# First sums ahead of the K/V matmuls, later norm sums, last stores in pairs of blocks: three small moves in a decoder layer on eight cores

## The chip, the cores and the metric

The kernel runs on the 8 cores of one Trainium2 chip (two dies, cores 0 to 3 and 4 to 7). Each core computes 1024 of the 8192 positions and does not talk to the others. The metric is the device time of the slowest core in microseconds (us). A run is called slow when one die is clearly longer at a lower granted TensorE clock.

A difference by dies below about half a us should not be read as more than the spread between chips. Most runs list the span and granted clock of every core. Where a size is quoted below "by dies", it is the mean span of the four cores of a die whose cores all had a granted clock of 0.997 or more in that execution (an undisturbed die), averaged over all such dies. For the kernel before this is 6568.96 us over 62 dies on several chips (62 of the 96 dies of its 48 executions with a list of cores; the other 34 had a lower clock), with a standard deviation of 0.44 us; the mean differed by at most 0.6 us from chip to chip. Dies of executions whose other die was slow are counted too, as long as their own clock was full.

## The reference, cut to what matters

```python
h = rms_norm(x, g0); z = h @ w_in            # q, k, v, pool input, two gates
...                                          # attention, pooling, output projection, conv MLP
ple_gate = sigmoid(rms_norm(x, g4) @ w_ple_gate)
x = x + rms_norm(ple_gate * (p @ w_ple), g5) # the last stage
```

Two pieces matter here. At the start, each core needs the sums of squares of its x (the norm) and the K and V projections. In the last stage, `rms_norm` needs a sum over all 4096 features before any output can be scaled, so this sum and what follows it stand at the very end.

## The kernel before: the parts that matter

One helper records every operation, in program order, onto one queue per engine; each engine then works through its queue in order. Waits are derived from the buffers read and written. So an operation that is queued early, and has to wait, holds up all that stands behind it on its engine: on VectorE the K/V eviction ran at 62.99 us behind a gain multiply that had stood 16.82 us for its x load (core 5, shown below).

The start. Positions come in 4 slices of 4 loads each (`g` counts 16 loads; the eight sum matmuls of load `g` are called one sum below, so the fifth sum is that of the first load of the second slice). `prep` squares a load on ScalarE and multiplies it by the gain on VectorE; `stat` sums the squares on TensorE (8 matmuls with ones); `kv` does 32 matmuls.

```python
def load_x(n):        # the sixth load waits until the last K/V weight piece has landed
    O("sp", "dma_start", [wkv[3][3].b] if n == 5 else [], [xsub[i].b], ...)
...
prep(0); prep(1)
for g in range(4 * NSL):
    s, q = g // 4, g % 4
    if q == 0:
        kv(g, 0, 4); stat(g); kv(g, 4, 8)
    else:
        stat(g); kv(g)
    prep(g + 2)
    if g < 4:
        ...                                  # two memsets on VectorE
    ...
    if q == 3:
        kv_evac(s)                           # VectorE takes K and V of the slice out of PSUM
```

The last stage. Matmuls are recorded one by one, and every so often one step of a side queue is recorded between two of them: `due` grows by 1/side for each matmul, and a step is taken when it reaches 1. The first half of the positions (512 wide) runs as 32 blocks, then the second half for 24 blocks, then the last 8 blocks as two quarters of 256 (`half_job`, h = 0 and 1). When a part is done, its norm is put into the side queue. Its first step is a sum on TensorE, which needs the last block's gate, product and square from VectorE and ScalarE.

```python
# end of the first half, in the last block's eviction
B.side.extend(last_A(acc_rstd(acc, ((0, 512),))))     # first step: norm sum, then 32 output steps
...
# last block of a quarter: gate, product, square, then
B.due = 0
B.side.extend(last_B(h, last_rstd(h), (t, ap, f)))    # first step: norm sum, Ln, Exp, scale, 3 copies
...
# the last quarter's output, by groups of 4 blocks
for i in range(2):
    O("dve", "tensor_tensor", [R.b, x.b], [R.b], ...)  # add the residual to two blocks
put(g)()                                               # store 4 blocks, 512 KB
...
for eng, b in final_waits:                             # at the end SyncE waits once for every store
    for k, v in b.w.items(): fin.append((eng, k, v))
```

The softmax here doesn't subtract the row's maximum and nothing guards it: scores larger than these inputs give would overflow.

## Time and profile before

| | us |
|---|---|
| time, first three runs | 6624.95, 6634.72, 7356.29 (slow) |
| profiled run, slowest core (5) | 6572.5 |
| TensorE busy | 6497.6 |
| wait for K/V weights at the start (core 5) | 30.8 |
| wait for VectorE before the fifth sum | 7.7 |
| wait before the first half's norm sum | 2.6 |
| wait before the third quarter's norm sum | 1.0 |
| last large matmul to the end | 29 |

The page of core 5: busy time of the engines, and the chain of work that ended last, by engine.

```profile
PE 6497.6 (99%) x41466; PEld 4044.5 (62%) x41466; DVE 2040.5 (31%) x2713; ACT 894.0 (14%) x1397; POOL 1355.0 (21%) x2554
...
PE 98%; DMA 1%; DVE 1%; issue 0%; ACT 0%; POOL 0%; DVEq 0%; ACTq 0%; POOLq 0%; SPq 0%
```

TensorE is the bound (99% busy, 98% of the chain), so only its gaps can be won. The timeline of the first 64 us (start, duration, engine, instruction, count, and in brackets the idle time before and what ended it):

```profile
32.03 3.37 PE L145 MATMUL ps<-sb_arena 128*128 128x296 bf16 x13 [6.19 <-DMA sb_arena<-w_in]
...
35.19 1.25 PE L145 MATMUL ps<-sb_arena,sb_ones_b 128*128 128x296 bf16 x8
...
58.24 2.36 DVE L145 TENSOR_SCALAR sb_arena<-sb_arena,sb_cf 128x296 bf16<-128x296 f32 x8 [16.82 <-DMA sb_arena<-xs]
...
62.99 4.61 DVE L145 TENSOR_TENSOR sb_arena<-ps,sb_arena 128x296 bf16<-128x296 f32 x10
...
63.54 2.13 PE L145 MATMUL ps<-sb_arena,sb_ones_b 128*128 128x296 bf16 x8 [7.71 <-DVE sb_arena L145]
```

The eight sums of the first load (35.19) run after the weights have come. The fifth sum (63.54) waits for the K/V eviction (62.99), which stands in VectorE's queue behind a gain multiply that waits for the sixth x load (58.24).

```profile
6295.00:6300.00 5.00, 3.44 (x16) 1.36 (x14) 1.38 (x2) 1.22 (x2) 1.61 (x3) 1.00 0.52 142
6300.00:6305.00 5.00, 3.95 (x10) 1.52 (x11) 0.69 (x1) 3.36 (x5) 0.54 (x1) 0.72 0.08 32
6305.00:6310.00 5.00, 5.00 (x23) 2.21 (x22) 2.91 (x5) 0.00 (x0) 1.07 (x2) 0.94 0.64 174
```

TensorE is empty for 2.61 us, and after that the granted clock of the stretch is 0.72: the 39 matmuls at 6301.98 took 10.27 us, where 39 at 0.215 us would be 8.4 (between 6240 and 6270 us, at full clock, two starts are 0.216 us apart on the mean). Two more sums:

```profile
6276.27 1.02 PE L145 MATMUL ps<-sb_arena,sb_ones_f 128*128 128x512 f32 x2
...
6483.09 0.67 PE L145 MATMUL ps<-sb_arena,sb_ones_f 128*128 128x256 f32 x2 [0.30 <-DVE sb_arena L145]
```

The sum at 6483.09 us is the first sum of the last 8 blocks.

The two quarters and the last block, on TensorE and VectorE:

```profile
6514.90 0.27 PE L145 MATMUL ps<-sb_arena,sb_ones_b 128*128 128x256 bf16 x1 [1.04 <-ACT sb_arena L145]
...
6520.57 0.27 PE L145 MATMUL ps<-sb_arena,sb_ones_b 128*128 128x256 bf16 x1
...
6549.13 0.70 DVE L145 COPY sb_arena<-sb_arena 128x256 f32<-128x256 f32 x3 [0.59 <-ACT sb_arena L145]
6549.93 18.80 DVE L145 TENSOR_TENSOR sb_arena<-sb_arena 128x1024 f32<-128x1024 f32 x24
```

Then the stores: issue of the last 8 and their time to landing, from the view of the output tensor after 6550 us.

```profile
L145 SPq DMA_DIRECT2D out<-sb_arena x8: 372/372/373, 6553.6 to 6568.9; - x8
...
DMA to landing us min/median/max: 3.0/3.0/3.3
```

### The profile page before, as it was taken

Reading aid. Unit: us, or ns where it says so; the run is one execution under the profiler, and the core shown is the slowest. Engines: PE = TensorE matmul, PEld = TensorE weight load, DVE = VectorE, ACT = ScalarE, POOL = GpSimd, SP = SyncE. Lnnn points to the kernel's source line nnn. Section 1 sums busy time; section 2 is a strip of 40 time slices with the busy share of each in tenths; the row PEclk is TensorE's granted clock in tenths of the full one; section 3 lists DMA queues with packets and bytes.
Section 4 is the critical chain, followed back from the end, with each engine's and each line's share of the span. In section 5 each row is a group of like instructions: output and inputs, shape, how many; then the busy total and the mean of one; then the engine's idle time right before and its main releaser. Section 6 shows DMA issues by size and latency. Waiting matters only on the chain.

```text
span 6572.5 us, 105521 instructions; the slowest of 8 cores (6566.5 to 6572.5 us)
## 1 busy us (share of the span) xinstructions
PE 6497.6 (99%) x41466; PEld 4044.5 (62%) x41466; DVE 2040.5 (31%) x2713; ACT 894.0 (14%) x1397; POOL 1355.0 (21%) x2554
## 2 busy tenths in 40 slices
PE   7999999999999999999999999999999999999998
PEld 5666666666665685866644566665456666544445
DVE  4443111111111236433300133332013333335654
ACT  3640000000001233000000000000000000013433
POOL 1111111111112332211111111111111111233333
PEclk9999999999999999999999999999999999999999
DMA  8568777777776678677799977446774544578888
GB/s 194 83 92 119 117 114 113 119 122 117 116 117 178 178 215 247 144 110 110 110 153 160 152 114 108 77 77 125 160 144 77 77 76 76 129 218 278 240 250 264
DMA packets 387829, 931.69 MB, mean 142 GB/s; under 512 B 50192, under 2 KB 89360, under 8 KB 381584
## 3 DMA queue, kind: packets, MB, share of 16 engines
q0 software_dynamic: 292576, 726.30, 62.2%
q1 hardware_dynamic: 94336, 197.94, 9.2%
q8 instruction: 339, 5.55, 0.3%
q14 instruction: 146, 1.20, 0.1%
q10 hardware_dynamic: 432, 0.70, 0.1%
HBM read 1318.44 MB, written 206.61 MB: 232 GB/s over the span
## 4 chain that ended last, share of the span: by engine, by line
PE 98%; DMA 1%; DVE 1%; issue 0%; ACT 0%; POOL 0%; DVEq 0%; ACTq 0%; POOLq 0%; SPq 0%
PE ps L145 98%; DVE sb_arena L145 1%; DMA sb_arena<-w_in 1%; ACT sb_arena L145 0%; POOL sb_arena L145 0%; DMA sb_wr<-b_pg 0%; DMA sb_arena<-xs 0%; DVEq L144 0%; ACT L145 0%; DVEq L133 0%; ACTq L144 0%; ACT sb_warm L145 0%; POOLq L144 0%; SPq L144 0%; POOLq L170 0%
## 5 line engine op out<-in xcount | busy, mean ns | idle before, releaser
L145 PE MATMUL ps<-sb_arena,sb_wr 128*128 128x512 bf16 (+5 forms) x40000 | 6370.4, 321 | 0.5 <-DMA sb_wr<-b_pg 0.3
L145 PEld LDWEIGHTS ps<-sb_arena,sb_wr 128*128 128x128 bf16 x40000 | 3905.1, 98 | 2381.7 <-issue 7.8
L145 DVE TENSOR_TENSOR sb_arena<-ps,sb_arena 128x512 f32<-128x512 f32 (+12 forms) x936 | 683.9, 733 | 3855.6 <-PE ps L145 3677.0
L145 ACT ACTIVATE sb_arena<-sb_arena 128x512 f32<-128x512 f32 (+11 forms) x727 | 501.8, 693 | 4545.4 <-DVE sb_arena L145 4437.6
L145 DVE TENSOR_TENSOR sb_arena<-sb_arena 128x512 f32<-128x512 f32 (+8 forms) x687 | 545.0, 815 | 512.0 <-ACT sb_arena L145 477.2
L145 POOL DMA_DIRECT2D sb_wr<-w_up x608 | 321.9, 529 | 1748.2 <-PE ps L145 1681.2
L145 DVE SCALAR_TENSOR_TENSOR sb_arena<-sb_arena,sb_cf 128x1024 f32<-128x1024 f32 (+4 forms) x512 | 546.2, 1067 | 40.8 <-DVE sb_arena L145 0.9
L145 POOL DMA_DIRECT2D sb_wr<-w_in x384 | 204.0, 532 | 1242.4 <-PE ps L145 1151.2
L145 POOL DMA_DIRECT2D sb_wr<-w_down x256 | 135.5, 529 | 666.1 <-PE ps L145 639.0
L145 ACT ACTIVATE sb_arena<-ps 128x512 bf16<-128x512 f32 (+8 forms) x299 | 162.8, 545 | 709.9 <-PE ps L145 696.9
L145 PE MATMUL ps<-sb_arena 128*128 128x296 bf16 (+4 forms) x1216 | 180.0, 267 | 33.9 <-DMA sb_arena<-w_in 30.8
L145 POOL DMA_DIRECT2D sb_wr<-b_out x256 | 137.4, 537 | 333.1 <-PE ps L145 309.0
L145 DVE TENSOR_SCALAR sb_arena<-sb_arena,sb_cf 128x1024 f32<-128x1024 f32 (+3 forms) x320 | 183.2, 602 | 59.2 <-DMA sb_arena<-xs 25.7
L145 POOL DMA_DIRECT2D sb_wr<-b_pg x288 | 154.6, 537 | 223.0 <-PE ps L145 195.5
L145 POOL DMA_DIRECT2D sb_wr<-b_down x256 | 137.4, 537 | 273.9 <-PE ps L145 236.6
L145 PEld LDWEIGHTS ps<-sb_arena 128*128 128x128 bf16 (+1 forms) x1216 | 113.6, 98 | 89.7 <-issue 51.0
L145 ACT ACTIVATE sb_arena<-sb_arena,sb_cf 128x512 bf16<-128x512 f32 (+3 forms) x224 | 146.3, 653 | 11.2 <-ACT sb_arena L145 2.0
L145 POOL DMA_DIRECT2D sb_wr<-b_up x160 | 86.1, 538 | 202.4 <-PE ps L145 189.9
L145 ACT ACTIVATE sb_arena<-ps,sb_cf 64x386 f32<-64x386 f32 (+3 forms) x112 | 69.9, 624 | 250.4 <-PE ps L145 247.9
L145 DVE TENSOR_TENSOR sb_arena<-sb_arena,sb_cb 128x512 bf16<-128x512 bf16 (+1 forms) x192 | 64.2, 335 | 45.7 <-ACT sb_arena L145 39.1
L145 POOL DMA_DIRECT2D sb_wr<-w_bp x64 | 33.8, 528 | 190.8 <-PE ps L145 190.8
L145 POOL DMA_DIRECT2D sb_wr<-w_ba x64 | 34.2, 534 | 171.8 <-PE ps L145 171.8
(32 smaller groups left out, 256.3 us busy)
## 6 DMA issues: line engine op xcount, KB each, us to landing
sb_wr<-w_up POOLq DMA_DIRECT2D x608, 256.0 KB, 4.0
sb_wr<-w_in POOLq DMA_DIRECT2D x384, 256.0 KB, 5.6
sb_wr<-b_pg POOLq DMA_DIRECT2D x288, 256.0 KB, 5.0
sb_wr<-b_out POOLq DMA_DIRECT2D x256, 256.0 KB, 3.0
sb_wr<-w_down POOLq DMA_DIRECT2D x192, 256.0 KB, 5.5
sb_wr<-b_down POOLq DMA_DIRECT2D x192, 256.0 KB, 3.7
sb_wr<-b_up POOLq DMA_DIRECT2D x160, 256.0 KB, 3.5
b_out<-w_out POOLq DMA_DIRECT2D x32, 1024.0 KB, 12.3
```

Source lines behind the costliest of these rows:

```text
L145: inst = getattr(engine, fn[0])(**fn[1])
```

## The change

Its intent: to use the empty time at the start for the first sums, to keep TensorE from waiting at two norm sums of the last stage, and to shorten the landing of the last store.

```diff
-            if q == 0:
+            if q == 0 and s > 0:
                 kv(g, 0, 4)
                 stat(g)
                 kv(g, 4, 8)
@@ end of the first half
+                    B.side.append(idle)
                     B.side.extend(last_A(acc_rstd(acc, ((0, 512),))))
@@ last block of a quarter
-                    B.due = 0
+                    B.due = -0.6
@@ stores
-            def put(g):
+            def put(g, i=0, n=4):
...
-                    O("sp", "dma_start", [R.b, tok], [b], dma=f"out{g % 8}",
-                      out=out_d[4 * g:4 * g + 4, :, c0:c0 + HW]..., in_=R.v)
+                    O("sp", "dma_start", [R.b, tok], [b], dma=f"out{(2 * g + i // 2) % 8}",
+                      out=out_d[f0:f0 + n, :, c0:c0 + HW]..., in_=R.v[:, i:i + n, :])
...
-                        put(g)()
+                        put(g, 0, 2)()
+                        put(g, 2, 2)()
```

`idle` is an empty step: it costs one turn of the side queue, 13 matmuls there.

## The prediction

> **What bounds the kernel.** TensorE. The page gives PE 6497.6 of 6572.5 us (99%), and the chain that ended last is 98% PE. PE is empty mainly at the two ends that the change touches: waits of 38.5 us near the start, and 29 us after the last large matmul (6543.1 us in the timeline). 2% would be 130 us.
>
> **First slice.** The waits of PE in 0 to 150 us are 30.8 us for the K/V weights (4 waits) and one of 7.7 us for VectorE. The first 8 sum matmuls now run at 34.9 to 36.2 us (1.25 us), after the weights of the fourth column block have landed (32.0 us). Their squares are ready by 13.5 us, so the change puts them into empty time, near 14 us. That frees 1.2 us of PE between 32 and 49.8 us. I expect it to be lost: the chain runs through the landing of the last weight piece (49.8 us), which releases the sixth x load, landing at 58.0 us, then VectorE's gain multiply, two memsets and the K/V eviction, and only then the next sums (63.54 us). Gain 0, at most 0.5 us.
>
> **Norm sums queued later.** (a) The sum of the first half waits 0.30 us for VectorE (6483.09 us). One empty step, 13 matmuls of 0.215 us, covers it: gain 0.3 us. (b) The sum of the third quarter waits 1.04 us for ScalarE (6514.90 us). Starting at -0.6 means 28 matmuls instead of 17 before it, 1.25 us more: the wait goes. But the chain behind it (Ln, Exp, three copies, the gate with a table load, square) does not start earlier, and the next-but-one sum needs that square (19.85 to 20.27 us). So I expect a new wait of about 0.8 us at the sum near 6520.5. From there on VectorE sets the pace: per block gate 0.42, gap 0.68, multiply plus two queued steps 2.7 to 2.8 us, 3.78 us on average against 3.76 of PE. One queued step fewer fits before the end (13 instead of 14 after the start), so the last gate comes up to 1.1 us earlier, but that step (1.13 us) is done after it, where 0.59 us was idle: net 0.5 us.
>
> **Stores in pairs.** Both halves still wait for both adds, so no byte leaves earlier, and the last 1 MB already moves at about 320 GB/s (3.3 us). SyncE issues 8 more stores (0.37 us each, hidden behind VectorE's 18.8 us of tail) and ends with 56 instead of 48 store waits at 0.05 us each, started 0.45 us later: this list (2.8 us) may then outlast the landing by about 0.3 us. Cost 0 to 0.5 us.
>
> **Sum.** 0.3 + 0.5 - 0.3, about 0.5 to 1 us less, 0.01%, below the spread between fast runs (6624.95 and 6634.72 us; 6574 us profiled). Predicted 6633 us, range 6580 to 6665; chances 0.02 faster, 0.96 same, 0.02 slower.
>
> **What would show it.** Right: sums near 14 us, yet PE's VectorE wait still ends near 63.5 us; no wait at the two moved sums, a wait of 0.5 to 1 us two sums later; copies of the last quarter's norm within 1 us of their old place; stores of 256 KB and a list of waits at the end. Wrong: a K/V eviction or last landing a microsecond earlier.
>
> **What would make it wrong.** Another order of transfers at the start; the clock (0.997 now); the slow state (7356 us in one run).

## More of the kernel before

The end of the first half, in the timeline and then in a table of stretches (busy time of PE, PEld, DVE, ACT and POOL, then the granted clock, DMA share and GB/s):

```profile
6300.21 0.69 DVE L145 TENSOR_TENSOR sb_arena<-sb_arena 128x512 f32<-128x512 f32 x1 [0.89 <-ACT sb_arena L145]
...
6301.05 1.10 PE L145 MATMUL ps<-sb_arena,sb_ones_f 128*128 128x512 f32 x2 [2.61 <-DVE sb_arena L145]
...
6301.98 10.27 PE L145 MATMUL ps<-sb_arena,sb_wr 128*128 128x512 bf16 x39
```

## The result, and the profile after

The kernel after took 6626.19 us (median of 5 runs, 6625.72 to 6758.24; a sixth execution, slow, took 7139.39). The kernel before had five runs beside it, the three above and two slow ones (7428.20 and 7767.61). The ratio of fast runs is 0.9995, with a 95% interval of 0.9971 to 1.0019: the same by the 2% rule. (Ratios are the mean time of one kernel's fast runs over that of the other's of the same rounds, so not quite the ratio of the medians quoted.) In all six executions die 0 had a clock of 0.990 or less (0.988 to 0.989 in the profiled run, where the clock record of core 0 has 335 us at 0.8125) and is not used here; die 1 was undisturbed in both profiles:

| core | 4 | 5 | 6 | 7 |
|---|---|---|---|---|
| span before, us | 6566.5 | 6572.5 | 6571.3 | 6566.5 |
| span after, us | 6562.1 | 6567.4 | 6567.2 | 6562.5 |

By dies the kernel after took 6565.11 us (5 dies, standard deviation 0.23), 3.85 us less than before. The prediction had 0.5 to 1 us.

The start of core 5 after:

```profile
12.67 2.13 PE L145 MATMUL ps<-sb_arena,sb_ones_b 128*128 128x296 bf16 x8 [12.67 <-DVE sb_arena L145]
...
57.89 2.36 DVE L145 TENSOR_SCALAR sb_arena<-sb_arena,sb_cf 128x296 bf16<-128x296 f32 x8 [18.46 <-DMA sb_arena<-xs]
...
62.64 4.61 DVE L145 TENSOR_TENSOR sb_arena<-ps,sb_arena 128x296 bf16<-128x296 f32 x10
...
63.19 2.13 PE L145 MATMUL ps<-sb_arena,sb_ones_b 128*128 128x296 bf16 x8 [7.45 <-DVE sb_arena L145]
```

The sums run at 12.67 us, yet the fifth sum starts at 63.19 instead of 63.54 us, with the same wait. The end of the first half:

```profile
6300.45 1.06 PE L145 MATMUL ps<-sb_arena,sb_ones_f 128*128 128x512 f32 x2
6301.35 28.87 PE L145 MATMUL ps<-sb_arena,sb_wr 128*128 128x512 bf16 x133
```

```profile
6295.00:6300.00 5.00, 5.00 (x25) 2.25 (x23) 1.80 (x3) 1.70 (x3) 2.14 (x4) 1.00 0.58 157
6300.00:6305.00 5.00, 5.00 (x22) 2.16 (x21) 0.82 (x2) 2.88 (x4) 1.07 (x2) 1.00 0.47 112
```

The gap is gone, and the clock stays at 1.00. The quarters:

```profile
6509.78 0.27 PE L145 MATMUL ps<-sb_arena,sb_ones_b 128*128 128x256 bf16 x1
...
6515.28 0.27 PE L145 MATMUL ps<-sb_arena,sb_ones_b 128*128 128x256 bf16 x1 [0.87 <-ACT sb_arena L145]
```

The wait of 1.04 us has left the moved sum and stands, at 0.87 us, before the sum after next. The stores:

```profile
L145 SPq DMA_DIRECT2D out<-sb_arena x12: 372/390/507, 6552.5 to 6563.5; - x12
...
DMA to landing us min/median/max: 2.2/2.9/3.0
```

The quickest store lands in 2.2 us instead of 3.0, the median one in 2.9 instead of 3.0, but this is no gain by itself. From VectorE's last add to the last byte there were 3.08 us before and 3.06 us after on core 5; from the last add to the end of the program 3.74 and 4.49 us.

### The profile page after: what moved, and what is told of

Its sections match the earlier page's. It is cut to its first block, busy times and chain, and to the rows that moved or that the text cites. A ratio compares the mean times of both kernels' runs of the same rounds, so it can differ in the third digit from the quotient of the medians.

```text
span 6624.3 us, 105543 instructions; the slowest of 8 cores (6562.1 to 6624.3 us)
## 1 busy us (share of the span) xinstructions
PE 6556.0 (99%) x41466; PEld 4060.0 (61%) x41466; DVE 2041.7 (31%) x2713; ACT 894.3 (13%) x1397; POOL 1359.8 (21%) x2554
## 4 chain that ended last, share of the span: by engine, by line
PE 98%; DMA 1%; DVE 1%; issue 0%; ACT 0%; POOL 0%; DVEq 0%; ACTq 0%; SPq 0%; POOLq 0%
PE ps L145 98%; DMA sb_arena<-w_in 1%; DVE sb_arena L145 1%; ACT sb_arena L145 0%; POOL sb_arena L145 0%; DMA sb_arena<-xs 0%; DVEq L144 0%; ACT L145 0%; DVEq L133 0%; ACTq L144 0%; SPq L144 0%; POOLq L170 0%
## 5 line engine op out<-in xcount | busy, mean ns | idle before, releaser
L145 DVE TENSOR_TENSOR sb_arena<-sb_arena 128x512 f32<-128x512 f32 (+9 forms) x687 | 545.0, 815 | 512.5 <-ACT sb_arena L145 477.7
```

Source lines behind the costliest of these rows:

```text
L145: inst = getattr(engine, fn[0])(**fn[1])
```

## The experiments

The theory after this comparison: the empty step won a wait and a low clock that followed it; the later start won a little; the first sums won nothing; the pairs cost about 0.7 us, through SyncE's list of waits at the end. All kernels below gave correct results.

### The four parts alone

Each run is the kernel before with one part of the diff above.

First sums alone:

```diff
-            if q == 0:
+            if q == 0 and s > 0:
```

> The kernel before, with only the first slice's 8 sum matmuls moved ahead of its K/V matmuls. Theory (the start runs through the landing of the last weight piece and of the sixth x load, then VectorE's queue): the sums run near 12 us, but the fifth sum still starts at 59.5 to 63.5 us as before (within 1 us on the mean of the cores of the fast die), and the span changes by less than 1 us. Rival (the 1.2 us taken off TensorE are kept): the fifth sum and everything after it come 1.2 us earlier on every core.

By dies: 6568.98 us over 7 dies, a difference of 0.02 us (standard error about 0.15). The fifth sum started at 60.8 us on the mean of the eight cores, against 61.6 us before, 60.9 with the empty step alone and 61.4 with the later start alone, which do not touch the start; cores differ by 4 us among themselves. The theory holds: the 1.2 us were not kept.

The empty step alone:

```diff
+                    B.side.append(idle)
                     B.side.extend(last_A(acc_rstd(acc, ((0, 512),))))
```

> The kernel before, with only the empty step ahead of the first half's norm sum. Theory (the wait of 2.6 us in front of that sum, near 6296 to 6301 us, goes, and with it the 3.41 us at half clock that follow it on some cores): 2.8 us less from the fifth sum to the last stage's half blocks on cores whose clock stayed up in the kernel before, 4.0 to 4.8 us less on cores whose clock fell; no half clock there any more. Rival (only the wait counts): 2.6 to 2.8 us less on every core.

By dies: 6565.10 us over 9 dies, 3.86 us less than before. This one line is as much as the whole change. A stretch that the start cannot disturb shows why: from the norm sum before (6276.27 us on core 5) to the first sum of the last 8 blocks (6483.09 us), the kernel before took 205.13 or 205.14 us on cores 4 and 7 and 206.82 us on cores 5 and 6. (Cores 0 to 3 had one more stretch there, 3.8 to 5.0 us at a clock of 0.8125, and are left out.) With the empty step it took 202.33 us on all eight cores (202.34 on one). Core 5 with the empty step:

```profile
6271.74 1.02 PE L145 MATMUL ps<-sb_arena,sb_ones_f 128*128 128x512 f32 x2
...
6296.56 1.06 PE L145 MATMUL ps<-sb_arena,sb_ones_f 128*128 128x512 f32 x2
...
6474.07 0.67 PE L145 MATMUL ps<-sb_arena,sb_ones_f 128*128 128x256 f32 x2 [0.29 <-DVE sb_arena L145]
```

So 2.80 us came from the wait, and another 1.69 us on those cores whose clock record shows 3.41 us at half clock behind it (half of 3.41 us is 1.71). The theory holds on both kinds of core, 2.80 us and 4.49 us, and the rival that only the wait counts does not.

The later start alone:

```diff
-                    B.due = 0
+                    B.due = -0.6
```

> The kernel before, with only the third quarter's norm sum queued 11 matmuls later. Theory (the wait moves to the sum after next, since ScalarE and VectorE behind it do not start earlier, and VectorE sets the pace to the end): the wait of 1.04 us goes, a new one of 0.8 to 0.9 us comes two sums later, the last quarter's copies come 0.5 to 1.0 us earlier relative to the first half block. Rival (the TensorE time won is kept): 1.0 us won already at the sum after next, with no new wait.

By dies: 6568.17 us over 8 dies, 0.79 us less. The wait of 1.04 us went, a wait of 0.87 us came two sums later on core 5, and from the first sum of the last 8 blocks to the last copies there were 65.4 us instead of 66.0. The gain is not the wait, which only moved: 48.7 us after that first sum, five sums after the moved one, both kernels are level again. It appears in the last four sums, which come 0.2, 0.4, 0.6 and 1.1 us earlier on core 5; before the copies VectorE no longer stands idle for 0.59 us, but has one more queued step to do there.

The pairs alone:

```diff
-                        put(g)()
+                        put(g, 0, 2)()
+                        put(g, 2, 2)()
```

> The kernel before, with only the last stores in pairs of blocks. Theory: from the end of VectorE's last add to the last byte of the store 3.0 to 3.2 us as before; to the end of the program 4.5 us, 0.6 to 0.8 us more than before (3.75 us), since SyncE's list of waits (56 instead of 48, and 0.5 us later) ends after the landing. Rival (smaller stores land sooner): the last byte lands 0.3 us or more earlier and the end follows it.

By dies: 6569.88 us over 8 dies, 0.92 us more than before. On the four undisturbed cores of its profile the last byte came 3.0 to 3.2 us after the last add, as before, and the end 4.5 us after it.

The four parts add up: 0.02 - 3.86 - 0.79 + 0.92 = -3.71 us, against -3.85 us measured for the whole. The baseline enters this sum four times: with the four undisturbed dies of before on the chip of these runs, in the same rounds (6569.15 us), the sum is -4.47. So the parts are shown to add up to within about 0.6 us, no better; that the empty step is by far the largest does not depend on the baseline.

### The wait and the clock: a smaller and a larger dose

```diff
+                    B.due -= 0.5       # instead of an idle step: 6 matmuls later
                     B.side.extend(last_A(acc_rstd(acc, ((0, 512),))))
```

> The kernel before, with the first half's norm sum queued 6 matmuls (1.29 us) later instead of 13. Theory (half clock follows only where one 3.41 us window of the clock record is idle for more than about half): the gap from the start of the matmul before to that sum falls from 2.98 to about 1.69 us; no half clock there on any of the 8 cores; from the sum before to the last stage's first half block 203.8 us on undisturbed cores (205.1 or 206.8 before, 202.33 with the empty step). Rival (a fall of the clock is as likely as the gap is long against the window, 81% before): half clock on 3 or 4 of 8 cores, and 205.5 us there.

```diff
+                    B.due = 0.95       # 4 matmuls earlier
                     B.side.extend(last_A(acc_rstd(acc, ((0, 512),))))
```

> The kernel before, with the same sum queued 4 matmuls (0.86 us) earlier, so that the gap grows from 2.98 to about 3.84 us. Theory: half clock for 3.41 us on all 8 cores (21 or 22 of 28 undisturbed ones so far at 2.98 us), and 207.7 us from the sum before to the first half block on every undisturbed core. Rival (the half clock there has another cause than the wait): about the same share of cores as before.

(The window of 3.41 us in the first expectation is a step of the clock record, shown below. "More than about half" was the estimate; what was measured is in the table below.)

The smaller dose did as expected on all eight cores: a gap of 1.69 us between starts, 203.84 or 203.85 us over the stretch, no half clock anywhere; by dies 6566.04 us (3 dies). The longer wait had a gap of 3.85 us, but half clock on 6 of 8 cores, not on all. Five of these took 207.68 to 207.70 us over the stretch, as the theory had it; core 6 had half clock for two windows, 6.83 us, and took 209.03. Cores 2 and 7 took 206.00 us and kept their clock. By dies it took 6569.99 us (4 dies). That is a miss of the theory in its simple form. Two cores of that one run, 5 and 2, in the table of stretches:

```profile
6300.00:6305.00 5.00, 4.48 (x11) 1.71 (x12) 0.81 (x2) 2.99 (x4) 0.00 (x0) 0.66 0.00 0
```

```profile
6300.00:6305.00 5.00, 4.28 (x18) 1.95 (x19) 0.81 (x2) 3.18 (x4) 0.54 (x1) 1.00 0.03 11
```

The clock column has 0.66 on core 5 and 1.00 on core 2, after the same wait.

The miss can be resolved from the clock records. In the profiles of before and after, the starts and ends of half clock on a core lie whole multiples of 3.413 us apart, to within 0.002 us on all 16 cores (the end of the last stretch is the end of the record and is left out), and the shortest stretch at half clock is one such step, 3.41 us. A step is called a window here. I took each core's fall of the clock at the end of the program as one window border, stepped back in steps of 3.413 us, and measured how much of the gap fell into a single window (the gap is counted from 0.215 us after the start of the matmul before the sum). This was done in nine profiles that have the gap, for all cores whose clock was otherwise full at that place, 70 in all:

| idle in one window, us | cores | half clock followed |
|---|---|---|
| 1.32 to 1.98 | 20 | 0 |
| 2.00, 2.07, 2.12 | 3 | 2 (not at 2.12) |
| 2.13 to 3.12 | 47 | 47 |

In every one of the 49 cases the half clock began at the end of that window. So it is not the length of the wait alone but how it lies across the windows: a wait of 3.6 us that a border cut in two near its middle (cores 2 and 7, 1.98 and 1.86 us in one window) was harmless, and one of 2.77 us that fell within one window was not. In these 70 cases the two kinds part between 1.98 and 2.13 us of idle time in one window. With the matmul ends that the profile models, 0.16 us later, they part with no exception: no half clock up to 1.98 us, half clock from 2.00 us on. This was found after these runs; no run was made that foretold it.

### What bounds the start

```diff
-            prep(g + 2)
-            if g < 4:
+            if q == 3:
+                ...                 # for g == 3 the last two memsets
+                kv_evac(s)
+            prep(g + 2)
+            if g < 3:
...
-            if q == 3:
-                kv_evac(s)
```

> The kernel before, with each slice's K/V eviction (and the last two memsets before the first one) put ahead of the next gain multiply in VectorE's queue. Theory (the wait at the first slice's end comes from VectorE's queue, whose head waits for the sixth x load): the fifth sum starts at 55 to 57 us instead of 59.5 to 63.5 us without a wait for VectorE; the sixth waits for the x load until about 59 to 60 us; the first ring-weight matmul comes 5 to 9 us earlier than the 122 us of before. Rival (the start is bound by the sum of x and weight transfers): the first ring-weight matmul moves by less than 2 us.

The fifth sum came at 54.1 to 55.5 us on all cores, with no wait for VectorE. But the time won was spent soon after. Core 5:

```profile
53.69 4.68 DVE L145 TENSOR_TENSOR sb_arena<-ps,sb_arena 128x296 bf16<-128x296 f32 x10 [10.06 <-PE ps L145]
...
55.49 1.17 PE L145 MATMUL ps<-sb_arena,sb_ones_b 128*128 128x296 bf16 x8
...
68.60 6.60 ACT L145 ACTIVATE sb_arena<-sb_arena 128x1184 bf16<-128x1184 f32 x6 [8.37 <-DMA sb_cf<-cf]
...
69.93 2.22 PE L145 MATMUL ps<-sb_arena,sb_ones_b 128*128 128x296 bf16 x8 [4.87 <-ACT sb_arena L145]
```

The fifth sum ran 8 us earlier than before (55.49 against 63.54), but a later sum waits 4.87 us for squares on ScalarE. The first matmul with ring weights (sb_wr, the first after the K/V stage) came at 120.0 us on the mean of eight cores, against 121.6 to 122.2 us in six runs that left the start as it was (before, empty step, later start, both doses, halves early). By dies it took 6566.72 us, 2.24 us less than before (7 dies, standard error 0.4). The theory was right on the fifth sum and the rival on the total, and it was tempting to stop there and call the start bound by its transfers.

The last two lines of the fence say otherwise: the wait of ScalarE ended with a transfer of constants (sb_cf), not of x. The seventh x load had landed at 62 us (VectorE took it at 62.13). ScalarE's queue stood still before the issue of the second load of constants, which wrote another tile but was recorded on the same buffer as the first, and so waited for the first to land.

```diff
-            O("act", "dma_start", [], [constB], partial=True, dma="cst2", out=cb[:], in_=cb_d)
-            for b in (gainB, onesB):
+            cbB = Buf("cb")
+            O("act", "dma_start", [], [cbB], dma="cst2", out=cb[:], in_=cb_d)
+            for b in (gainB, onesB, cbB):
```

> The kernel with the eviction first, and in addition the second load of constants no longer made to wait for the first one to land (it wrote another tile, but both were recorded on one buffer). In the eviction run ScalarE's queue stood still for 8.4 us at that issue (58.3 to 68.1 us on core 5), before the squares of the seventh x load, which had landed at 62 us. Theory (that stop, not the transfers, took the eviction's gain back): the seventh sum starts at 63 to 66 us instead of 69.9 us (65.7 and 64.9 us on the quicker cores 0 and 4), and the first ring-weight matmul comes at 113 to 117 us on the mean of the cores instead of 120.0. Rival (the start is bound by its transfers): 119 us or later.

The seventh sum came at 62.0 to 64.9 us, as the theory had it, and the first ring-weight matmul at 119.2 us, as the rival had it. By dies 6566.68 us (3 dies), the same as without it, with the half clock of the section above on all eight cores here and on five in the run before. The next stop, core 5 again:

```profile
71.81 4.86 DVE L145 MEMSET sb_arena<- 128x5760 bf16 x1 [1.15 <-issue]
76.68 4.68 DVE L145 TENSOR_TENSOR sb_arena<-ps,sb_arena 128x296 bf16<-128x296 f32 x10
```

The second slice's eviction stands behind a memset of 4.86 us, and TensorE waited 2.7 us for it here (2.7 to 3.9 us on the three cores looked at). The last run of this chain is told below, with all that helped in it.

One thing is left open: in the runs with the eviction first the gap before the first half's norm sum was 0.35 us longer than before on all cores (3.33 us between starts), since one VectorE product started later, though the recorded order at that place is the same.

### What the pairs cost

```diff
...                                          # the bookkeeping of waits is moved below this
+        top = {}
+        for eng, k, v in fin:
+            top[eng, k] = max(v, top.get((eng, k), 0))
+        fin = [(eng, k, v) for (eng, k), v in top.items()]
```

> The kernel after, with one final wait for each semaphore instead of one for each store (8 instead of 56). Theory (the pairs cost only the length of SyncE's list of waits): from VectorE's last add to the end 3.75 us or a little less (4.49 us after, 3.75 us before); last byte at 3.0 to 3.1 us as in both. Rival (the smaller stores themselves are slower): 4.2 us or more.

From the last add to the end 3.68 to 4.18 us, mean 3.81 us, and by dies 6564.11 us, 1.00 us less than the kernel after (5 dies each). The last byte came at 3.03 to 3.15 us as before. So it was the list of 56 waits, not the stores. In the semaphore records of the kernel after, this list runs from 6564.02 to 6567.14 us, while the last byte had landed at 6565.99 us. A wait that was already met took about 0.05 us: in the list of the kernel before, 40 waits start between 6569.28 and 6571.22 us.

Then the pairs as they can help: each pair leaves after its own add. This run is the kernel before with these stores and with the short list.

```diff
                     for i in range(2):
+                        half = Buf(f"half{h}{g}{i}")
-                        O("dve", "tensor_tensor", [R.b, x.b], [R.b], ...)
-                    if h == 1:
-                        put(g)()
+                        O("dve", "tensor_tensor", [R.b, x.b], [R.b, half], ...)
+                        if h == 1:
+                            put(g, 2 * i, 2, half)()
```

> The kernel before, with the last quarter's stores in pairs of blocks, each issued after its own add and not after both, and with one final wait for each semaphore. Theory (pairs gain only if a half may leave before the second add): from VectorE's last add to the last byte about 2.3 to 2.6 us instead of 3.1, to the end about 3.0 to 3.3 us instead of 3.75. Rival (the last megabyte is bound by bandwidth alone): 3.0 us and 3.7 us as before.

The last byte came 2.43 to 2.53 us after the last add, and the end 3.07 to 3.48 us after it (about 3.3 on the mean), so the theory holds in the tail. On core 5 a store of 256 KB landed in 2.5 us as a median, against 2.9 us for the pairs issued one behind the other in the kernel after and 3.0 us for the 512 KB of before. The spans do not show it (6569.05 us by dies, 2 dies): in its profile all eight cores had the half clock described above, against five of eight in the profile of before.

### All that helped, together

First sums, eviction first, empty step, later start, halves after their own add, short list.

> All that helped, together: first sums ahead, eviction ahead in VectorE's queue, the empty step, the later start, halves of the last stores each after its own add, and the short list of waits. Theory (the parts add up): 203 us or less from the sum before to the last stage's first half block with no half clock, the wait of 0.87 us after the moved sum as in the kernel after, 3.0 to 3.3 us from the last add to the end; slowest core of an undisturbed run near 6564 us, against 6572 us before and 6567 us after. Rival (the gains overlap): 6567 us or more.

It took 6566.14 to 6567.56 us in its five fast runs; the fast runs of before in the same rounds took 6572.96 to 6575.37 us. The ratio of fast runs is 0.9989, with an interval of 0.9974 to 1.0005. By dies it took 6562.13 us (12 dies), 6.83 us less than before. The stretch across the first half's norm sum took 202.68 or 202.69 us with no half clock; the 0.35 us above 202.33 are the open point of the eviction run. The end came 3.16 us after the last add on the mean.

The same with the constants' load unlinked:

> All that helped, with the same change of the constants' load. Theory: by dies what the constants' load gains in the run beside this one comes off the 6562.1 us of all that helped (3 to 7 us). Rival: 6561.5 us or more by dies.

By dies 6560.19 us (7 dies), 8.77 us less than before; two fast runs took 6564.19 and 6564.28 us. The step of 1.94 us is neither the 3 to 7 us of the theory nor nothing: the next stop had taken most of it.

The same with the memset moved into VectorE's idle time:

```diff
-            if g == 6:
+            if g == 1:
                 O("dve", "memset", [], [va.b], ap=va.v.rearrange("p a b -> p (a b)"), constant=1.0)
```

> All that helped with the constants' load unlinked, and in addition the 4.86 us memset of the V tile on VectorE moved from ahead of the second slice's eviction to the idle time near 30 us. In the run before it, TensorE's last wait at the start was 2.7 to 3.9 us for that eviction, which stood behind the memset. Theory (the start is bound by what stands in VectorE's and ScalarE's queues, one thing after another): that wait shrinks below 1 us, and the first ring-weight matmul comes 2 to 3.5 us earlier than the 118.8 us of the kernel without it; by dies 6557 to 6558.5 us. Rival (by now the x transfers bind): the wait turns into one for x or its squares, and by dies 6559.5 us or more.

The first ring-weight matmul came at 113.8 us on the mean of eight cores, 5.0 us earlier than in the run before and 8.4 us earlier than in the kernel before. By dies it took 6555.52 us (8 dies, standard deviation 0.23): 13.44 us less than the kernel before and 9.59 us less than the kernel after, and more than the theory had expected. From 50 us to the first ring weight, core 5's TensorE has no wait longer than this one:

```profile
59.30 0.66 PE L150 MATMUL ps<-sb_arena,sb_ones_b 128*128 128x296 bf16 x4 [0.42 <-ACT sb_arena L150]
```

A second reason for the size of this gain is the clock, in the records of the same profiles. In the kernel before, every core had half clock for 6.8 or 10.2 us (on core 5 from 59.23 us), around the wait for VectorE; in the run before this one six of eight cores had one window of it, near 80 us; with the memset moved no core had any between its first matmuls at full clock and its last. Core 5 from 60 to 80 us, before and now (the columns as above; the clock is the one before the last two):

```profile
60.00:80.00 20.00, 16.46 (x108) 11.71 (x109) 18.21 (x40) 7.06 (x7) 0.00 (x0) 0.76 0.81 264
```

```profile
60.00:80.00 20.00, 20.00 (x160) 15.21 (x159) 12.22 (x37) 11.19 (x12) 0.00 (x0) 1.00 0.98 330
```

Half of TensorE's busy time at half clock is 2.35 us on the mean of eight cores in the kernel before, 1.24 us in the run before this one, and nothing now (an estimate from the clock records and the matmuls in them). So about 1.2 of the 5.0 us are clock and not wait.

So after the weights had landed the start was not bound by its transfers. It was bound by three operations in the queues of VectorE and ScalarE, one behind the other, and each of them hid the next. The two runs with the whole chip undisturbed took 6558.63 and 6559.02 us, against 6573.79 to 6575.15 us for the fast runs of before in the same rounds. The ratio over all fast runs is 0.9995 (0.9951 to 1.0038), since one fast run, 6582.93 us, had cores 6 and 7 at a clock of 0.993 to 0.994; by the 2% rule it is the same. By dies it is the version that beats both kernels. What the first sums are worth in a start without these stops was not tried.

## Why the prediction was right or wrong

In the large the prediction held: no change by the 2% rule. That 6626.19 us lies in its range is luck: the time is that of die 0, whose clock was 0.988, while the cores of die 1 took 6562 to 6567 us. In the later rounds 19 of 20 fast runs of before took 6573 to 6575 us, below the range of 6580 to 6665. The size of the gain did not hold: 3.85 us by dies instead of 0.5 to 1. Point by point:

- **First sums, "Gain 0, at most 0.5 us": right.** Alone they moved the time by 0.02 us, and the fifth sum kept its wait, for the reason given: the chain through the sixth x load and VectorE's queue. Of that chain it was the order in the queue that could be changed, and behind it stood two more stops of the same kind.
- **Empty step, "The sum of the first half waits 0.30 us for VectorE (6483.09 us)": wrong, and this is the step that failed.** The sum at 6483.09 us is the first of the running sums of the last 8 blocks. Its wait is still there after the change (0.29 us at 6477.97 us). The first half's norm sum stood 182 us earlier, at 6301.05 us, with a wait of 2.61 us. I had that wait in the list of TensorE's gaps and took it for another sum, because I found the sum by its shape and the wait by its place near the end. Following the diff to the instruction (the first step after the 32nd block of the first half) would have shown it. The empty step won 2.80 us of wait, and 1.69 us of low clock where the clock had fallen; 3.86 us by dies.
- **The low clock was missing from the sum.** The page of before shows a clock of 9 tenths or more in all its slices; a stretch of 5 us shows 0.72, and one of 20 us at the start 0.76. A gap on the bounding engine was costed at its own length.
- **Later start: right in mechanism.** A new wait of "about 0.8 us" two sums later was 0.87 us, the last gate came 1.1 us earlier as foretold, and the gain of 0.5 us was 0.79 us by dies (0.7 us at the copies).
- **Pairs: right in mechanism, too small.** The last byte came no earlier, and the list of waits outlasted it. The term "by about 0.3 us" measured 0.75 us on core 5's tail and 0.92 us by dies. The list took 3.12 us instead of the estimated 2.8, with a pause of 0.35 us in its middle whose cause no view shows.
- The terms were -0.3, -0.5 and +0.3 us; they measured -3.86, -0.79 and +0.92 us.

## What to carry to other kernels

Trace each line of a diff to the very instruction it moves before you read a wait off the profile: two sums of the same kind, 182 us apart, had waits of 2.6 and 0.3 us. On the bounding engine, cost a gap together with the clock that follows it (here 2.80 us of wait, and 1.69 us of low clock where the clock had fallen): look at short stretches, not at the whole. Where an engine that is not the bound holds the bound up through the order of its queue, expect a second such stop behind the first (here there were three): take them away one by one before calling the stretch bound by transfers.
